# A decoder trunk on one core: gate-and-up operands built in place on VectorE, memory work at the head of the FFNs, other groups in the down projection

## The chip, the cores and the metric

The kernel runs on one core of one Trainium2 chip. The metric is the device time of one execution in microseconds; the time before is the median of three runs. Inputs and outputs are fp32.

## The reference

Two layers. Each has four sub-layers with an RMS norm before and after it: an FFN, a token mixer, a cross-attention into 256 memory tokens, and a second FFN. T is 512 tokens, the model width is 1024, the FFN's inner width 2816. Cut to what the change touches:

```python
def swiglu(x, w_gate, w_up, w_down):
    return (jax.nn.silu(x @ w_gate) * (x @ w_up)) @ w_down

for l in range(DEPTH):
    y = swiglu(rms_norm(x, ffn1_pre_g[l]), ffn1_w_gate[l], ffn1_w_up[l], ffn1_w_down[l])
    x = x + 0.5 * rms_norm(y, ffn1_post_g[l])
    y = hybrid_mixer(rms_norm(x, mix_pre_g[l]), ...)
    x = x + rms_norm(y, mix_post_g[l])
    y = memory_xattn(rms_norm(x, xa_pre_g[l]), rms_norm(mem, xa_mem_g[l]), ...)
    x = x + rms_norm(y, xa_post_g[l])
    y = swiglu(rms_norm(x, ffn2_pre_g[l]), ffn2_w_gate[l], ffn2_w_up[l], ffn2_w_down[l])
    x = x + 0.5 * rms_norm(y, ffn2_post_g[l])
```

## The kernel before, in words

**Layout and products.** All activations are kept transposed: eight tiles `x[0..7]` of 128 features by 512 tokens. An fp32 product is made of three matmuls in a rounded fp32 format: both operands are split into a high and a low part, and `mm3` (L119) adds high by high (L121), high weight by low x (L122) and low weight by high x (L123) in one PSUM bank. A weight unit is 128x1024: SyncE loads it raw, ScalarE copies the high part `whi` (L88), VectorE subtracts to get the low part `wlo` (L89). There are six raw buffers and four each of `whi` and `wlo`; four PSUM banks for accumulators and four for other uses.

**The FFN.** 22 blocks of 128 inner features are worked off as 11 pairs (class `Pair`, L325). Pairs 0 and 1 are plain: gate and up of each block, all eight x tiles (`plain`). Pairs 2 to 10 replace eight block products by seven, as Strassen's scheme does: the x side is cut into four blocks (two halves of the features by two halves of the tokens), and products 1 to 7 use x blocks or their differences and sums (operands `ops[o, k]`), with weight combinations that are loaded ready, or made by adding a second load onto the first: an accumulate-DMA issued on GpSimd's queue (L341, four per pair). The operands 1 to 4 are plain halves of x, 5 to 8 are built once per FFN in `combos` (L221), after the first plain pair: a 128x256 difference on VectorE, one on GpSimd, again one each, for four rows k; the high and low parts of operands 7 and 8 are made in a second loop over k. Their high parts have a buffer of their own, the rest comes from pool "xs" with 24 buffers.

The seven products run in the order p1, p5, p2, p7, p6, p4, p3. Each is 24 matmuls of 256 columns. Between them VectorE and GpSimd form the sums of the results: after p6 `e = B - s1` (L420, VectorE) and `s5 = e - s5` (L421, GpSimd); after p4 `s7 = e - s7` (L425) and `s5 = s5 - C` (L426), both on VectorE. `swiglu` then makes the gated product of both blocks and splits it (L132, L133).

**The down projection** goes in groups of blocks. When the list `hs` holds four finished blocks at the end of a pair's products, `down` runs them: for each of eight output tiles, 12 matmuls of 512 columns, and VectorE adds the bank to `y[c]` (L485). So groups of four run after pairs 2, 4, 6, 8 and 10, and a last group of two at the end. In the last FFN of the kernel the last group runs in two halves of 256 tokens (`down_halves`), so that the output of the first half leaves while the second is computed. In a last group the squares of y are added up as they come (`sumsq`, L161), on GpSimd for all tiles but the last, which is VectorE's.

**Between stages.** `postnorm` turns the sum of squares into a row of factors: a transposing matmul into `rms_ps` (L169), a reduction (L171), a short Newton iteration on VectorE in 128x4 operations (L139 to L148), a broadcasting matmul into `bc_ps` (L185). Then x is updated tile by tile and split anew for the next stage (`x1h`, L211). Where the next stage is an FFN, `postnorm` calls `nxt[0]()` first (L274): it runs that FFN's `filler`, if there is one (`mem_keys`, the cross-attention keys of the next layer, whose units run on TensorE as `ps_mk`), and splits the first two gate and up units. `ffn_first` (L446) makes this closure and leaves the pairs in `warm` for `ffn` (L457). Keys 0 to 3 of layer 1 ride ahead of ffn2 of layer 0, keys 4 to 7 ahead of ffn1 of layer 1.

**What sets the order.** A scheduler lists the instructions of each engine once, when the kernel is built, in the program's order as far as their inputs are ready in its own model; each engine then runs its list in order. A DMA is issued by the engine whose queue it is in, so an accumulate-DMA stands in GpSimd's list among its additions. A tile is reused when all that read it are done.

Of the kernel before, what the change touches and what calls it, by code (L numbers as in the profile page):

```python
# [9 lines left out]
F32 = mybir.dt.float32  # L10
F32R = mybir.dt.float32r
# [36 lines left out]
def trunk(ctx: ExitStack, tc: tile.TileContext, a: dict, out: bass.AP):  # L48
# [11 lines left out]
    def big(name, dt=F32, shape=(P, T), tag="b"):  # L60
        return bp.tile(list(shape), dt, name=name, tag=tag, bufs=slots[tag])
# [158 lines left out]

    def combos(g):  # L221

        sums = []
        h7 = big("x7h", F32R, shape=(P, 4, T), tag="onsa")

        def put(o, k, t, hi, lo):
            act.activation(hi, t, AF.Copy)
            dve.tensor_tensor(lo, t, hi.bitcast(F32), op=ALU.subtract)
            for u in range(2):
                ops[o + u, k] = hi[:, HALVES[u]], lo[:, HALVES[u]]  # L230

        for k in range(4):
            b = []
            for c in (k, k + 4):
                xg = big("xg")
                act.activation(xg, x[c], AF.Copy, scale=g[:, c : c + 1])
                b += [xg[:, HALVES[0]], xg[:, HALVES[1]]]
            t5, t7 = big("xt"), big("xt")
            dve.tensor_tensor(t5[:, :256], b[1], b[0], op=ALU.subtract)
            pool.tensor_tensor(t7[:, :256], b[3], b[1], op=ALU.subtract)  # L240
            dve.tensor_tensor(t5[:, 256:], b[3], t5[:, :256], op=ALU.subtract)
            pool.tensor_tensor(t7[:, 256:], t5[:, 256:], b[2], op=ALU.subtract)
            put(5, k, t5, big("x5h", F32R, tag="xs"), big("x5l", F32R, tag="xs"))
            sums.append(t7)
        for k in range(4):
            put(7, k, sums[k], h7[:, k], big("x7l", F32R, tag="xs"))

    def gcols(l, col):
        return small[l][:, col : col + NC]
# [20 lines left out]
    def postnorm(y, ssq, gains, nxt, ts_=slice(0, T), cols=None):  # L270


        w = ts_.stop - ts_.start
        if ts_.start == 0 and nxt[0]:  # L274
            nxt[0]()
        ps = row_bc(rms_cols(ssq[:, ts_], D, w, cols), w // P)
        for c in range(NC):
            t = big("yn")[:, :w]
            dve.scalar_tensor_tensor(t, y[c][:, ts_], gains[:, c : c + 1], ps, op0=ALU.mult, op1=ALU.mult)
            (dve if c == 0 else pool).tensor_tensor(x[c][:, ts_], x[c][:, ts_], t, op=ALU.add)  # L280
            (split_s if nxt[0] else split_x)(c, nxt[1], ts_)
# [16 lines left out]
    def out_halves(src, l, oh, ol, gains, nxt):  # L298

        y, ssq, w = [], None, {}  # L300
        for c in range(NC):
            wh, wl = unit(src[l, c], 1024)
            y.append(big("y"))
            if c >= NC - 2:
                w[c] = wh, wl
                continue
            ps = acc("ps_o")
            for k in range(NC):
                s = slice(k * P, (k + 1) * P)
                mm3(ps, wh[:, s], wl[:, s], oh[k], ol[k], k == 0, k == NC - 1)  # L310
            ssq = sumsq(ssq, ps, c, pool)
            dve.tensor_copy(y[c], ps)
        for ts_ in HALVES:
            for c in w:
                ps = acc("ps_o")[:, : T // 2]
                for k in range(NC):
                    s = slice(k * P, (k + 1) * P)
                    mm3(ps, w[c][0][:, s], w[c][1][:, s], oh[k][:, ts_], ol[k][:, ts_], k == 0, k == NC - 1)
                sq = big("sq")[:, : T // 2]
                act.activation(sq, ps, AF.Square)  # L320
                dve.tensor_tensor(ssq[:, ts_], ssq[:, ts_], sq, op=ALU.add)
                dve.tensor_copy(y[c][:, ts_], ps)
            postnorm(y, ssq, gains, nxt, ts_)

    class Pair:  # L325

# [118 lines left out]
    warm = {}  # L445

    def ffn_first(l, which, filler=None):

        def run():
            if filler:  # L450
                filler()
            ps_ = warm[l, which] = [Pair(a[FF_UNITS[which][0]][l], j) for j in range(NPAIR)]
            for q in range(2):
                ps_[0].w["q", q] = split_unit(ps_[0].load(q))
        return run

    def ffn(l, which, gains, nxt, prep=None):  # L457
        dn = FF_UNITS[which][1]
        pairs = warm.pop((l, which))
        y, state = [None] * NC, {"ssq": None}  # L460
        ORDER = "p1", "p5", "p2", "p7", "p6", "p4", "p3"

# [12 lines left out]
        def down(f0, hs, final):  # L475
            n = len(hs)
            for c, w in weights(f0, n):
                ps = acc("ps_dn")
                for k in range(n):
                    mm3(ps, *w[k], *hs[k], k == 0, k == n - 1)  # L480
                if f0 == 0:
                    y[c] = big("y")
                    act.activation(y[c], ps, AF.Copy)
                else:
                    dve.tensor_tensor(y[c], ps, y[c], op=ALU.add)  # L485
                if final:
# [7 lines left out]
        for p in pairs[:2]:  # L494
            for f in range(2):
                p.plain(f, bc, hs)
                if p is pairs[0] and f == 1:
                    combos(gcols(l, G_F1PRE if which == "ffn1" else G_F2PRE))
        f0 = 0
        for p in pairs[2:]:  # L500
            final = p is pairs[-1]
            for n in ORDER:
                getattr(p, n)()
            mine = []
            if len(hs) == 4:
                down(f0, hs, False)
                f0, hs = f0 + 4, []
            p.swiglu(bc, hs, "xs" if final else "h")
        if prep:
            prep()  # L510
        if nxt is None:
# [523 lines left out]
        mem_norm()  # L1035
        mem_split(0)

    ffn_first(0, "ffn1")()
    for c in range(NC):
        split_s(c, gcols(0, G_F1PRE))  # L1040
    ffn(0, "ffn1", half1[0], (None, gcols(0, G_MIXPRE)), prep=first_prep)
    mixer(0, (None, gcols(0, G_XAPRE)), filler=keys(0, 0, 7), prep=split_mem(0))
    xattn(0, (ffn_first(0, "ffn2", keys(1, 0, 4)), gcols(0, G_F2PRE)), filler=lambda: (mem_keys(0, 7, 8), mem_values(0, 0)), mid=values(0, 1), prep=split_mem(1))
    ffn(0, "ffn2", half2[0], (ffn_first(1, "ffn1", keys(1, 4, 8)), gcols(1, G_F1PRE)), prep=split_mem(1))
    ffn(1, "ffn1", half1[1], (None, gcols(1, G_MIXPRE)), prep=split_mem(1))
    mixer(1, (None, gcols(1, G_XAPRE)), filler=values(1, 0), prep=split_mem(1))
    xattn(1, (ffn_first(1, "ffn2"), gcols(1, G_F2PRE)), filler=values(1, 1), halves=True)
    ffn(1, "ffn2", half2[1], None)


# [90 lines left out]
```

## Time and profile before

| | us |
|---|---|
| median of three runs | 2546.82 (2544.16 to 2546.93) |
| the profiled execution | 2542.61 |
| its span, first to last instruction | 2540.8 |
| TensorE busy | 2402.8 |
| VectorE busy | 1696.1 |
| ScalarE busy | 1101.6 |
| GpSimd busy | 461.6 |

The profile is of one execution. A row of the timeline reads: start, duration, engine, line, operation, the tile written and those read, shapes and count; in brackets the time the engine sat idle before it and what ended that. PE is TensorE, DVE VectorE, ACT ScalarE, POOL GpSimd. PEclk is the granted clock of TensorE in tenths of full speed, 9 being 0.9 or more in a slice; in a table of stretches it is a share. Matmuls are pipelined: one row's duration is longer than the distance to the next.

### The profile page before, as it was taken

Reading aid. Unit: us, or ns where it says so; the run is one execution under the profiler, and the core shown is the slowest. Engines: PE = TensorE matmul, PEld = TensorE weight load, DVE = VectorE, ACT = ScalarE, POOL = GpSimd, SP = SyncE. Lnnn points to the kernel's source line nnn. Section 1 sums busy time; section 2 is a strip of 40 time slices with the busy share of each in tenths; the row PEclk is TensorE's granted clock in tenths of the full one; section 3 lists DMA queues with packets and bytes.
Section 4 is the critical chain, followed back from the end, with each engine's and each line's share of the span. In section 5 each row is a group of like instructions: output and inputs, shape, how many; then the busy total and the mean of one; then the engine's idle time right before and its main releaser. Section 6 shows DMA issues by size and latency. Waiting matters only on the chain.

```text
span 2540.8 us, 37896 instructions
## 1 busy us (share of the span) xinstructions
PE 2402.8 (95%) x14860; PEld 2132.7 (84%) x14860; DVE 1696.1 (67%) x3018; ACT 1101.6 (43%) x1760; POOL 461.6 (18%) x430
## 2 busy tenths in 40 slices
PE   8999988999999989999989999989999997999996
PEld 7999977888878879999879999868888776999995
DVE  7566687465777485666885666774657766756666
ACT  6443443255345354444454444422553443544442
POOL 2111123001040131111231111230010403211112
PEclk9999998999999999999989999989999998999998
DMA  6766642411232336666526666514112322367661
GB/s 209 166 161 163 165 151 67 143 51 52 74 104 95 100 78 164 164 160 159 160 80 163 167 167 160 149 58 142 51 51 68 100 67 75 98 162 166 165 163 35
DMA packets 107523, 309.59 MB, mean 122 GB/s; under 512 B 10448, under 2 KB 24016, under 8 KB 107344
## 3 DMA queue, kind: packets, MB, share of 16 engines
q1 hardware_dynamic: 77392, 222.21, 26.7%
q0 software_dynamic: 20736, 75.51, 17.7%
q10 hardware_dynamic: 9216, 9.44, 1.2%
q8 instruction: 117, 1.92, 0.3%
q14 instruction: 62, 0.51, 0.1%
HBM read 305.02 MB, written 2.10 MB: 121 GB/s over the span
## 4 chain that ended last, share of the span: by engine, by line
PE 43%; DVE 5%; issue 2%; DMA 2%; ACT 2%; POOL 1%; POOLq 0%; ACTq 0%; DVEq 0%
PE ps_gu L121 4%; PE ps_gu L122 4%; PE ps_gu L123 4%; PE ps_dn L121 3%; PE ps_dn L122 3%; PE ps_dn L123 3%; DMA raw<-in_ffn_gu_dram 2%; PE ps_po L829 1%; PE ps_gc L121 1%; PE ps_gc L123 1%; PE ps_gc L122 1%; PE ps_o L121 1%; PE ps_o L122 1%; PE ps_o L123 1%; PE ps_fm L123 1%
## 5 line engine op out<-in xcount | busy, mean ns | idle before, releaser
L89 DVE TENSOR_TENSOR wlo<-raw,whi 128x1024 fp32r<-128x1024 f32 (+1 forms) x506 | 619.7, 1231 | 410.6 <-ACT whi L88 408.2
L88 ACT ACTIVATE whi<-raw 128x1024 fp32r<-128x1024 f32 (+1 forms) x506 | 529.5, 1054 | 797.3 <-DMA raw<-in_ffn_gu_dram 185.5
L341 POOL DMA_DIRECT2D raw<-in_ffn_gu_dram x144 | 125.7, 891 | 974.9 <-DVE wlo L89 730.4
L121 PE MATMUL ps_dn<-hh,whi 128*128 128x512 f32 (+1 forms) x720 | 277.5, 385 | 1.2 <-DVE y L485 1.2
L122 PE MATMUL ps_dn<-hl,whi 128*128 128x512 f32 (+1 forms) x720 | 277.3, 385 | 0.0
L123 PE MATMUL ps_dn<-hh,wlo 128*128 128x512 f32 (+1 forms) x720 | 277.3, 385 | 0.0
L121 PE MATMUL ps_gu<-x3h,whi 128*128 128x256 f32 (+1 forms) x704 | 216.7, 308 | 24.9 <-ACT gk L375 24.9
L122 PE MATMUL ps_gu<-x3l,whi 128*128 128x256 f32 (+1 forms) x704 | 215.6, 306 | 1.2 <-DVE x3l L218 1.2
L161 POOL TENSOR_TENSOR ssq<-ssq,sq 128x512 f32<-128x512 f32 (+1 forms) x84 | 130.3, 1552 | 469.1 <-ACT sq L160 465.6
L123 PE MATMUL ps_gu<-x3h,wlo 128*128 128x256 f32 (+1 forms) x704 | 215.0, 305 | 0.0
L121 PE MATMUL ps_gu<-x1h,whi 128*128 128x256 f32 x544 | 158.1, 295 | 24.8 <-ACT x1h L211 11.0
L121 PE MATMUL ps_gc<-x7h,whi 128*128 128x256 f32 x576 | 163.3, 283 | 0.9 <-ACT gk L375 0.9
L121 PEld LDWEIGHTS ps_gu<-x3h,whi 128*128 128x128 f32 x704 | 136.6, 194 | 32.7 <-ACT gk L375 28.2
L121 PE MATMUL ps_gu<-x5h,whi 128*128 128x256 f32 x576 | 163.0, 283 | 0.0
L122 PE MATMUL ps_gu<-x5l,whi 128*128 128x256 f32 x576 | 163.0, 283 | 0.0
L123 PE MATMUL ps_gc<-x7h,wlo 128*128 128x256 f32 x576 | 163.0, 283 | 0.0
L122 PE MATMUL ps_gc<-x7l,whi 128*128 128x256 f32 x576 | 163.0, 283 | 0.0
L123 PE MATMUL ps_gu<-x5h,wlo 128*128 128x256 f32 x576 | 162.9, 283 | 0.0
L122 PE MATMUL ps_gu<-x1l,whi 128*128 128x256 f32 x544 | 158.6, 292 | 1.2 <-DVE x1l L212 1.0
L121 PEld LDWEIGHTS ps_dn<-hh,whi 128*128 128x128 f32 x720 | 135.5, 188 | 28.0 <-DVE y L485 1.6
L123 PEld LDWEIGHTS ps_dn<-hh,wlo 128*128 128x128 f32 x720 | 135.5, 188 | 27.1
L123 PE MATMUL ps_gu<-x1h,wlo 128*128 128x256 f32 x544 | 158.0, 292 | 0.2
(267 smaller groups left out, 5997.6 us busy)
## 6 DMA issues: line engine op xcount, KB each, us to landing
raw<-in_ffn_gu_dram SPq DMA_DIRECT2D x176, 512.0 KB, 4.1
raw<-in_ffn_gu_dram POOLq DMA_DIRECT2D x144, 512.0 KB, 5.7
raw<-in_ffn_dn_dram SPq DMA_DIRECT2D x88, 512.0 KB, 4.2
raw<-in_win_fm_dram SPq DMA_DIRECT2D x32, 512.0 KB, 3.6
raw<-in_wk_dram SPq DMA_DIRECT2D x16, 512.0 KB, 3.8
raw<-in_cmp_w_dram SPq DMA_DIRECT2D x16, 512.0 KB, 4.1
raw<-in_wout_dram SPq DMA_DIRECT2D x16, 512.0 KB, 3.3
raw<-in_wv_dram SPq DMA_DIRECT2D x16, 512.0 KB, 3.3
```

The costliest lines, as they stand in the source:

```text
L88: act.activation(hi, raw, AF.Copy)
L89: dve.tensor_tensor(lo, raw, hi.bitcast(F32), op=ALU.subtract)
L121: pe.matmul(ps, ah, bh, start=start, stop=False, skip_group_check=more)
L122: pe.matmul(ps, ah, bl, start=False, stop=False, skip_group_check=more)
L123: pe.matmul(ps, al, bh, start=False, stop=stop, skip_group_check=more)
L161: eng.tensor_tensor(acc_t, acc_t, sq, op=ALU.add)
L341: pool.dma_start(t, self.quarter(q), accum_op=ALU.add)
L829: pe.matmul(po[:, i], blk[i, j], vsel[j // 2][:, j % 2, col : col + DH], start=j == 0, stop=j == i)
```

## The change

- `combos`: all four differences of a row are made on VectorE and in place, in the two tiles that held the scaled x; the four blocks of the first tile become operands 5 and 7, those of the second 8 and 6. Both are split in the same turn of the loop, so no second loop.
- `p6`: `s5 = e - s5` is on VectorE.
- `ffn_first` and `warm` go; `ffn` takes the filler and runs it at its head, before its own norm rows, after the postnorm of the stage ahead. The splits of the first two units are made in `plain` like all others; the kernel's first two units alone are split ahead, through `cut`, among the first splits of x. The first entry of `nxt` becomes a flag for how x is split.
- The squares of a last group are added on VectorE for odd tiles and on GpSimd for even ones (not in `down_halves`).
- A down group also runs with two blocks in hand after pair 3, and, where another stage follows, after pair 10. So the groups of three FFNs are 4, 2, 4, 4, 4, 2, 2 (after pairs 2, 3, 5, 7, 9, 10 and at the end), and of the last FFN 4, 2, 4, 4, 4, 4, the last in halves.

```diff
 def combos(g):
-    sums = []
-    h7 = big("x7h", F32R, shape=(P, 4, T), tag="onsa")
-    def put(o, k, t, hi, lo):
-        act.activation(hi, t, AF.Copy)
-        dve.tensor_tensor(lo, t, hi.bitcast(F32), op=ALU.subtract)
-        for u in range(2):
-            ops[o + u, k] = hi[:, HALVES[u]], lo[:, HALVES[u]]
+    hb = big("x8h", F32R, shape=(P, 4, T), tag="onsa")
     for k in range(4):
...
-        t5, t7 = big("xt"), big("xt")
-        dve.tensor_tensor(t5[:, :256], b[1], b[0], op=ALU.subtract)
-        pool.tensor_tensor(t7[:, :256], b[3], b[1], op=ALU.subtract)
-        dve.tensor_tensor(t5[:, 256:], b[3], t5[:, :256], op=ALU.subtract)
-        pool.tensor_tensor(t7[:, 256:], t5[:, 256:], b[2], op=ALU.subtract)
-        put(5, k, t5, big("x5h", F32R, tag="xs"), big("x5l", F32R, tag="xs"))
-        sums.append(t7)
-    for k in range(4):
-        put(7, k, sums[k], h7[:, k], big("x7l", F32R, tag="xs"))
+        xg = [big("xg") for _ in range(2)]
+        for c, t in zip((k, k + 4), xg):
+            act.activation(t, x[c], AF.Copy, scale=g[:, c : c + 1])
+        b1, b2, b3, b4 = [t[:, u] for t in xg for u in HALVES]
+        for o, i, j in ((b1, b2, b1), (b2, b4, b2), (b4, b4, b1), (b3, b4, b3)):
+            dve.tensor_tensor(o, i, j, op=ALU.subtract)
+        for t, hi, o in ((xg[0], big("x5h", F32R, tag="xs"), (5, 7)), (xg[1], hb[:, k], (8, 6))):
+            lo = big("x5l", F32R, tag="xs")
+            act.activation(hi, t, AF.Copy)
+            dve.tensor_tensor(lo, t, hi.bitcast(F32), op=ALU.subtract)
+            for u in range(2):
+                ops[o[u], k] = hi[:, HALVES[u]], lo[:, HALVES[u]]
@@ postnorm
-    if ts_.start == 0 and nxt[0]:
-        nxt[0]()
@@ plain
-            k0 = "q", 2 * f + q
-            wh, wl = self.w.pop(k0) if k0 in self.w else split_unit(self.load(2 * f + q))
+            k0 = self.j, 2 * f + q
+            wh, wl = cut.pop(k0) if k0 in cut else split_unit(self.load(2 * f + q))
@@ p6
-        pool.tensor_tensor(self.s5, self.e, self.s5, op=ALU.subtract)
+        dve.tensor_tensor(self.s5, self.e, self.s5, op=ALU.subtract)
@@ ffn (ffn_first and warm are removed)
-def ffn(l, which, gains, nxt, prep=None):
+def ffn(l, which, gains, nxt, filler=None, prep=None):
+    if filler:
+        filler()
+    pairs = [Pair(a[FF_UNITS[which][0]][l], j) for j in range(NPAIR)]
...
-            state["ssq"] = sumsq(state["ssq"], y[c], c, dve if c == NC - 1 else pool)
+            state["ssq"] = sumsq(state["ssq"], y[c], c, dve if c % 2 else pool)
...
-        if len(hs) == 4:
+        if len(hs) == 4 or len(hs) == 2 and (p is pairs[3] or p is pairs[-1] and nxt is not None):
             down(f0, hs, False)
-            f0, hs = f0 + 4, []
+            f0, hs = f0 + len(hs), []
@@ the calls
-xattn(0, (ffn_first(0, "ffn2", keys(1, 0, 4)), gcols(0, G_F2PRE)), ...)
-ffn(0, "ffn2", half2[0], (ffn_first(1, "ffn1", keys(1, 4, 8)), gcols(1, G_F1PRE)), prep=split_mem(1))
-ffn(1, "ffn1", half1[1], (None, gcols(1, G_MIXPRE)), prep=split_mem(1))
+xattn(0, (True, gcols(0, G_F2PRE)), ...)
+ffn(0, "ffn2", half2[0], (True, gcols(1, G_F1PRE)), filler=keys(1, 0, 4), prep=split_mem(1))
+ffn(1, "ffn1", half1[1], (False, gcols(1, G_MIXPRE)), filler=keys(1, 4, 8), prep=split_mem(1))
```

## Rows read from the trace of the kernel before

**Rows 1.** The page: busy time of the engines, and granted clock in 40 slices.

```profile
PE 2402.8 (95%) x14860; PEld 2132.7 (84%) x14860; DVE 1696.1 (67%) x3018; ACT 1101.6 (43%) x1760; POOL 461.6 (18%) x430
...
PEclk9999998999999999999989999989999998999998
```

**Rows 2.** Waits of TensorE: us in total, times, longest us.

```profile
PE ps_gu L121 <- ACT gk L375: 24.9, 16, 2.3
PE bc_ps L185 <- DVE rs_y L148: 12.8, 11, 4.3
```

**Rows 3.** Stretches of 40 us at two changes of stage: busy us by engine, clock.

```profile
880.00:920.00 40.00, 30.90 (x200) 28.33 (x199) 31.89 (x48) 18.40 (x28) 16.01 (x11) 0.87 0.34 97
...
1280.00:1320.00 40.00, 31.18 (x182) 27.54 (x183) 33.94 (x65) 18.23 (x31) 16.22 (x12) 0.83 0.25 69
```

**Rows 4.** Timeline ahead of one wait of TensorE in pair 4 of an FFN.

```profile
1075.97 2.18 DVE L425 TENSOR_TENSOR gk<-ge,gk 128x512 f32<-128x512 f32 x1
1075.98 1.62 POOL L421 TENSOR_TENSOR gk<-ge,gk 128x512 f32<-128x512 f32 x1
...
1078.08 1.21 DVE L89 TENSOR_TENSOR wlo<-raw,whi 128x1024 fp32r<-128x1024 f32 x1
...
1079.60 0.88 POOL L341 DMA_DIRECT2D raw<-in_ffn_gu_dram  x1 [2.00 <-DVE wlo L89]
1079.82 1.21 DVE L89 TENSOR_TENSOR wlo<-raw,whi 128x1024 fp32r<-128x1024 f32 x1
...
1085.48 1.06 ACT L88 ACTIVATE whi<-raw 128x1024 fp32r<-128x1024 f32 x1 [2.20 <-DMA raw<-in_ffn_gu_dram]
...
1088.12 0.39 PE L121 MATMUL ps_gu<-x3h,whi 128*128 128x256 f32 x1 [2.13 <-ACT gk L375]
```

**Rows 5.** VectorE's subtraction L425: min/median/max ns; its sum, mean; the wait for L421.

```profile
L425 DVE TENSOR_TENSOR gk<-ge,gk x36: 678/1739/2198, 72.8 to 2476.4; 128x512 f32<-128x512 f32 x36
...
L425 DVE TENSOR_TENSOR gk<-ge,gk 128x512 f32<-128x512 f32 x36 | 52.0, 1444 | 0.5
...
  POOL gk L421: 37.1, 15
```

**Rows 6.** Accumulate-DMA issues on GpSimd's queue: duration of an issue, min/median/max ns.

```profile
L341 POOL DMA_DIRECT2D raw<-in_ffn_gu_dram x144: 862/865/1197, 29.7 to 2466.5; - x144
```

**Rows 7.** Timeline from the last square to the first gate product of ffn2, layer 0.

```profile
882.89 0.68 DVE L161 TENSOR_TENSOR ssq<-ssq,sq 128x512 f32<-128x512 f32 x1
...
892.20 0.60 PE L169 MATMUL rms_ps<-cst,ssq 128*128 128x128 f32 x4
...
900.32 1.01 PE L121 MATMUL ps_gu<-x1h,whi 128*128 128x256 f32 x3 [2.64 <-ACT x1h L211]
```

**Rows 8.** The same ahead of ffn1, layer 1.

```profile
1269.79 0.69 DVE L161 TENSOR_TENSOR ssq<-ssq,sq 128x512 f32<-128x512 f32 x1 [1.19 <-POOL ssq L161]
...
1277.66 0.60 PE L169 MATMUL rms_ps<-cst,ssq 128*128 128x128 f32 x4
...
1288.10 1.23 PE L121 MATMUL ps_gu<-x1h,whi 128*128 128x256 f32 x4 [4.16 <-ACT x1h L211]
```

**Rows 9.** Timeline of the last group in halves, and the wait behind it.

```profile
2502.77 0.28 PE L121 MATMUL ps_dn<-hh,whi 128*128 128x256 f32 x1
...
2514.96 0.28 PE L123 MATMUL ps_dn<-hh,wlo 128*128 128x256 f32 x1
...
2518.50 0.72 ACT L160 ACTIVATE sq<-y 128x256 f32<-128x256 f32 x2 [6.87 <-POOL x L532]
...
2527.02 0.69 PE L169 MATMUL rms_ps<-cst,ssq 128*128 128x128 f32 x2 [10.38 <-DVE ssq L161]
```

**Rows 10.** Gating of pair 10 in the last FFN: its first sum and its last copy.

```profile
2481.19 0.69 DVE L431 TENSOR_TENSOR ge<-ps_gu,ge 128x512 f32<-128x512 f32 x1 [0.17 <-PE ps_gu L123]
...
2490.43 0.63 ACT L132 ACTIVATE hh<-g 128x512 fp32r<-128x512 f32 x1 [2.81 <-DVE g L442]
```

**Rows 11.** A wait of TensorE for a weight split in the first mixer.

```profile
403.98 0.58 PE L123 MATMUL ps_mk<-memg,wlo 128*128 128x256 f32 x1 [3.10 <-DVE wlo L89]
```

More of the change, by code (lines that the diff above doesn't have):

```diff
@@ L221, in combos @@
     def combos(g):
-        sums = []
-        h7 = big("x7h", F32R, shape=(P, 4, T), tag="onsa")
-        def put(o, k, t, hi, lo):
-            act.activation(hi, t, AF.Copy)
-            dve.tensor_tensor(lo, t, hi.bitcast(F32), op=ALU.subtract)
-            for u in range(2):
-                ops[o + u, k] = hi[:, HALVES[u]], lo[:, HALVES[u]]
-        for k in range(4):
[L233 to L237, printed above, removed]
-            t5, t7 = big("xt"), big("xt")
-            dve.tensor_tensor(t5[:, :256], b[1], b[0], op=ALU.subtract)
-            pool.tensor_tensor(t7[:, :256], b[3], b[1], op=ALU.subtract)
-            dve.tensor_tensor(t5[:, 256:], b[3], t5[:, :256], op=ALU.subtract)
-            pool.tensor_tensor(t7[:, 256:], t5[:, 256:], b[2], op=ALU.subtract)
-            put(5, k, t5, big("x5h", F32R, tag="xs"), big("x5l", F32R, tag="xs"))
-            sums.append(t7)
-        for k in range(4):
-            put(7, k, sums[k], h7[:, k], big("x7l", F32R, tag="xs"))
+        hb = big("x8h", F32R, shape=(P, 4, T), tag="onsa")
+        for k in range(4):
+            xg = [big("xg") for _ in range(2)]
[10 more added lines that the diff above has]
+                    ops[o[u], k] = hi[:, HALVES[u]], lo[:, HALVES[u]]
     def gcols(l, col):
@@ L323, in out_halves @@
             postnorm(y, ssq, gains, nxt, ts_)
+    cut = {}
     class Pair:
@@ L443, in swiglu @@
                 hs.append(split(g1, "h", 0.5, tag=tag))
[L445 to L455, printed above, removed]
-    def ffn(l, which, gains, nxt, prep=None):
+    def ffn(l, which, gains, nxt, filler=None, prep=None):
+        if filler:
+            filler()
+        pairs = [Pair(a[FF_UNITS[which][0]][l], j) for j in range(NPAIR)]
         dn = FF_UNITS[which][1]
-        pairs = warm.pop((l, which))
         y, state = [None] * NC, {"ssq": None}
@@ L496, in ffn @@
                 p.plain(f, bc, hs)
-                if p is pairs[0] and f == 1:
-                    combos(gcols(l, G_F1PRE if which == "ffn1" else G_F2PRE))
+            if p is pairs[0]:
+                combos(gcols(l, G_F1PRE if which == "ffn1" else G_F2PRE))
         f0 = 0
         for p in pairs[2:]:
-            final = p is pairs[-1]
             for n in ORDER:
                 getattr(p, n)()
-            mine = []
-            if len(hs) == 4:
+            if len(hs) == 4 or len(hs) == 2 and (p is pairs[3] or p is pairs[-1] and nxt is not None):
                 down(f0, hs, False)
-                f0, hs = f0 + 4, []
-            p.swiglu(bc, hs, "xs" if final else "h")
+                f0, hs = f0 + len(hs), []
+            p.swiglu(bc, hs, "xs" if p is pairs[-1] else "h")
         if prep:
@@ L1036, in first_prep @@
         mem_split(0)
-    ffn_first(0, "ffn1")()
-    for c in range(NC):
+    cut[0, 0] = split_unit(first.pop((0, 0)))
+    for c in range(4):
         split_s(c, gcols(0, G_F1PRE))
-    ffn(0, "ffn1", half1[0], (None, gcols(0, G_MIXPRE)), prep=first_prep)
-    mixer(0, (None, gcols(0, G_XAPRE)), filler=keys(0, 0, 7), prep=split_mem(0))
-    xattn(0, (ffn_first(0, "ffn2", keys(1, 0, 4)), gcols(0, G_F2PRE)), filler=lambda: (mem_keys(0, 7, 8), mem_values(0, 0)), mid=values(0, 1), prep=split_mem(1))
-    ffn(0, "ffn2", half2[0], (ffn_first(1, "ffn1", keys(1, 4, 8)), gcols(1, G_F1PRE)), prep=split_mem(1))
-    ffn(1, "ffn1", half1[1], (None, gcols(1, G_MIXPRE)), prep=split_mem(1))
-    mixer(1, (None, gcols(1, G_XAPRE)), filler=values(1, 0), prep=split_mem(1))
-    xattn(1, (ffn_first(1, "ffn2"), gcols(1, G_F2PRE)), filler=values(1, 1), halves=True)
+    cut[0, 1] = split_unit(first.pop((0, 1)))
+    for c in range(4, NC):
+        split_s(c, gcols(0, G_F1PRE))
+    ffn(0, "ffn1", half1[0], (False, gcols(0, G_MIXPRE)), prep=first_prep)
+    mixer(0, (False, gcols(0, G_XAPRE)), filler=keys(0, 0, 7), prep=split_mem(0))
+    xattn(0, (True, gcols(0, G_F2PRE)), filler=lambda: (mem_keys(0, 7, 8), mem_values(0, 0)), mid=values(0, 1), prep=split_mem(1))
+    ffn(0, "ffn2", half2[0], (True, gcols(1, G_F1PRE)), filler=keys(1, 0, 4), prep=split_mem(1))
+    ffn(1, "ffn1", half1[1], (False, gcols(1, G_MIXPRE)), filler=keys(1, 4, 8), prep=split_mem(1))
+    mixer(1, (False, gcols(1, G_XAPRE)), filler=values(1, 0), prep=split_mem(1))
+    xattn(1, (True, gcols(1, G_F2PRE)), filler=values(1, 1), halves=True)
     ffn(1, "ffn2", half2[1], None)
```

## The prediction

> **What bounds the kernel now.** I read the page's busy shares first: TensorE is busy 95% of the span, VectorE 67%, GpSimd 18% [rows 1]. So only what leaves TensorE waiting, or what adds to its work, can move the time: 2540.8 − 2402.8 = 138 us of the span is idle TensorE. The slice line shows that the granted clock is at 0.8 to 0.9 in a few slices, which are the changes of stage. Then the waits of TensorE: the largest group is the gate and up product that waits for ScalarE's copy of a PSUM bank, 24.9 us in 16 waits; the normalisation's last VectorE step costs another 12.8 us in 11 [rows 2]. Then stretches of 40 us around the stage changes: 30.9 and 31.2 us of TensorE in 40, at a granted clock of 0.87 and 0.83, with VectorE at 32 and 34 us [rows 3]. There VectorE is nearly as full as TensorE. Last the timelines around each.
>
> **Rows 4 are one of the 16 waits, followed back.** TensorE stops for 2.13 us at 1088.12. The product it starts needs a PSUM bank that ScalarE frees late, because ScalarE had waited 2.20 us for an accumulated weight tile (1085.48). That tile's accumulate-DMA was issued by GpSimd at 1079.60, after VectorE's split at 1078.08, and that split stood behind one VectorE subtraction that took 2.18 us beside a GpSimd subtraction of 1.62 us. Alone the same subtraction takes 0.68 us; its mean is 1.44 [rows 5]. All 16 waits come at the third product of pairs 4, 6, 8 and 10, each of them after a pair at whose end no down group ran: a down group gives the loads 22 us of slack, a pair without one gives none.
>
> **The change part by part.** *(1) s5 on VectorE.* 36 subtractions leave GpSimd. VectorE takes on 36 × 0.68 = 24 us and loses what the collision cost it, 36 × (1.44 − 0.68) = 27 us [rows 5]. Its waits for the GpSimd result, 37.1 us in 15 [rows 5], go. So VectorE's load is about even and its delay smaller: in the chain of rows 4 the split comes 2.18 − 0.68 = 1.5 us earlier, less 0.68 if the moved subtraction stands ahead of it, so 0.8 to 1.5 earlier. How much of a wait of 1.55 us (24.9 / 16) that takes is open, since the DMA's landing (5.9 us from issue to use here) varies too: 0 to all of it; I take a third, 0.5 us. Nothing on GpSimd queues behind anything then: between the accumulate issues its list is empty.
>
> The Trainium skill, page "SBUF — State Buffer", section "SBUF: two separate sides", says that VectorE (with two SBUF inputs) and GpSimd share a port pair as an exclusive lock, and that a DMA issued from GpSimd's queue can be starved of its descriptors while VectorE holds it. Its first half agrees with the 2.18 us above; its second half speaks against this part, since it puts another two-input VectorE operation beside the accumulate issues. The trace of before doesn't show that: the issue at 1079.60 took 0.88 us beside the split of 1079.82, which reads two SBUF tiles, and over all 144 the median is 0.865 and the longest 1.197 [rows 4, 6]. By the rule each of some 12 waits would be up to 0.68 us longer, +8 us, and the sum would come to 2531; by the rows it stays.
>
> *(2) Down groups.* 22 blocks went as 4,4,4,4,4,2 after pairs 2, 4, 6, 8, 10 and the end. Now three FFNs go 4,2,4,4,4,2,2, after pairs 2, 3, 5, 7, 9, 10 and the end, and the last goes 4,2,4,4,4 and then 4 in halves. So "two blocks larger" holds for the last group of the last FFN alone. Pairs without a group before them are then 5, 7 and 9 in an FFN: three waits in place of four, and 4 × 1.55 = 6.2 us go. With part 1's 12 × 0.5 = 6 the sum is **−12**, bounds 0 (the waits only move) and −25 (all go). The number of weight loads is the same; the extra group adds 8 y additions, 8 × 0.68 = 5.5 us of VectorE beside a TensorE that runs.
>
> The other side of it is the end of the first three FFNs. After the last product, the block's gating takes from 2481.19 to the copy at 2490.43, some 10.6 us with the second split behind it, and today hides under a group of four blocks, 2481 to 2502.8, 21.8 us [rows 9, 10]. After the change it has a group of two, 10.9 us, in which VectorE must do 8 y additions instead of the 4 that half of the longer group brings, 4 × 0.68 = 2.7 us more. So the last group waits 10.6 + 2.7 − 10.9 = 2.4 us in each: **+7**, bounds 0 and +15 (5 each: the preparation of the next stage queues there too).
>
> *(3) Memory work to the head of FFNs.* Of the key work, 96 matmuls run between out-projection and the transpose of ffn2(0)'s post-norm. The sum of squares is ready at 883.6 and its transpose runs at 892.20 only, so 8.6 us are lost; the first gate product starts at 900.32 after waits of 4.3 (the normalisation, the longest of [rows 2]) and 2.64 us [rows 7]. At the head of the FFN, the transpose goes at 883.7 and the same matmuls can fill the waits behind it. What then is late is VectorE: the splits of the key weights and of the first gate units, 1.22 us each, come behind the norm instead of beside the matmuls, and four of these units' worth, less what the norm leaves open, is 2.5 us. I take 8.5 − 2.5 = **−6**, bounds 0 and −8.5. Before ffn1(1) it's the same: ready at 1270.5, transpose at 1277.66, first product at 1288.10 after 4.16 [rows 8]; 7.2 less 2.2 is **−5**, bounds 0 and −7.2. The last FFN had no such matmuls: 0 ± 3 there.
>
> *(4) Tail.* In the last FFN the final group of two in halves lasts from 2502.77 to 2515.2. The second half's squares wait 6.87 us on ScalarE for buffers that the first half's output still holds, and the transpose comes 10.38 us after the last product [rows 9]. With halves of four blocks the second half lasts 11.5 us instead of 5.8, the output of the first ends within it, and the transpose comes some 2 to 2.5 us after the last product, −8 to −9.5 with a little shorter queue. Against it: the last group no longer hides pair 10's gating, which without y additions (2.7) and weight splits (two, 2.4) lasts 10.6 − 5.1 = 5.5 us. The blocks of pair 9 give 24 matmuls that can go before, in four PSUM banks, at 0.12 us each 2.9 us; so 2.6 are lost, and I add 1 for a lower clock after the wait, as the slices at stage changes have it. **−5.5**, bounds −9.5 and +3.
>
> *(5) Differences in place.* Eight subtractions of 128x256 per FFN move from GpSimd to VectorE; not over 0.68 us each [rows 5], 5.5 us per FFN, beside the matmuls of the plain pairs. The third and fourth block rows get buffers that the first pair frees; by my count they're ready 4 us before product 5 wants them. **0**; without that cover one wait per FFN, of 2 us as in rows 4, +8. *(6) Squares alternate in the final group*: the VectorE addition at 1269.79 [rows 8] waited 1.19 us for GpSimd; it's in the −5. *(7) The start* is the same work in nearly the same order: **0**.
>
> Sum against the profiled execution (2542.6, span 2540.8 and 1.8 around it): −12 + 7 − 6 − 5 − 5.5 = −21.5, so 2521.1. That execution lies 4.2 under the median of the runs, 2546.8; a median of after may lie either way, so I add half: **2523 us**.
>
> **The rivals.** *A. VectorE becomes the bound at stage changes (slower).* It is at 34 us of 40 there already [rows 3], and where in an earlier stage such splits queued behind the norm, TensorE waited 3.10 us in one place [rows 11]. Then the transitions give 0, the ends of FFNs cost their +15, each of 12 waits becomes 1.55 + 0.68 = 2.2 (26.9 in place of 24.9, +2), and only the tail's −5.5 stays: +11.5, **2556**. It decides where the last group's second block is split over 5 us after TensorE wants it. Against it: VectorE's total hardly grows.
>
> *B. The moved memory matmuls were no cost.* If the chain of normalisation and not TensorE's order sets the start of the next FFN, the transitions give 0: −10.5, **2534**. For it: after the transpose the wait is VectorE's. Against: the sum of squares stands ready 8.6 and 7.2 us.
>
> *C. The groups do not do what their name says and the waits move only.* In three of four FFNs the last group stays at two blocks, and the one ahead of it shrinks. If pairs 5, 7 and 9 wait as long in sum as 4, 6, 8 and 10 did and the transitions give a quarter, the sum is 0 + 7 − 2.8 − 5.5 = −1.3, **2543**.
>
> *D. All waits of rows 4 vanish*, because only the collision made the load late: −25 in place of −12: 2508 to 2510, **2509**.
>
> **How the numbers follow.** My forecast, 2512 to 2534, has 0.53; D 0.11, B 0.10, C 0.12 and A 0.14. A difference under 0.2% (5 us) can't be told from none: C lies there, and so does the upper edge of B. Faster is 0.53 + 0.11 + 0.09 (of B) = 0.73, within it 0.01 + 0.12 = 0.13, slower 0.14. The range runs from 2503, just under D, to 2553, into A.
>
> **What would show it.** Part 1: VectorE's subtraction at 0.68 us throughout, no waits for GpSimd's, and the group of 16 waits shrinks to 12 under 1.1 us each, at pairs 5, 7, 9; wrong if the sum stays at 25. Part 2: a wait for the split of the last block just ahead of each final group, 2 to 3 us in three FFNs; A if over 5. Part 3: the transpose within 1 us of the sum of squares, the first gate product of ffn2(0) and ffn1(1) 5 to 6 us earlier counted from the last product before; B if not. Part 4: the end comes about 16 us after the last product, not 25.6. The prediction is wrong if VectorE stands full beside an idle TensorE for over 10 us at any of these places, or if the first seven-product pair waits for its differences.

## The result, and the profile after

The changed kernel takes 2521.57 us, median of four runs (2520.18 to 2530.73), against 2545.88 for the kernel before beside it (2544.16 to 2546.93): ratio 0.9913, interval 0.9888 to 0.9937. The forecast was 2523. The profiled execution took 2522.7, span 2520.9. A second set on another chip gives 2517.92 against 2539.74, 0.9917 (0.9903 to 0.9930); that kernel is called *changed again* below.

The page of the changed kernel, busy shares, and then its waits of TensorE (columns as in [rows 1, 2]); the last line is the group that led, in *changed again*:

```profile
PE 2405.7 (95%) x14908; PEld 2134.0 (85%) x14908; DVE 1703.9 (68%) x3119; ACT 1102.9 (44%) x1760; POOL 368.5 (15%) x353
```

```profile
PE ps_gu L121 <- ACT gk L365: 12.3, 12, 1.9
...
PE rms_ps L169 <- DVE ssq L161: 7.5, 3, 3.7
...
PE bc_ps L185 <- DVE rs_y L148: 4.3, 9, 2.3
```

```profile
PE ps_gu L121 <- ACT gk L365: 9.7, 12, 1.7
```

TensorE does 3 us more work than before and VectorE 8 us more; what went is idle time. The group that led the waits [rows 2] is halved, 24.9 us in 16 to 12.3 in 12, and the norm's step to a third. To see where the rest went, I cut each execution at marks that all have: the first matmul of product 7 in an FFN, its last down product, and the end. This is worked out from TensorE's rows in the timelines; the columns are the kernel before, the changed one, the changed one again, and a variant of the experiments (4,4,4,4,4,2 in the first three FFNs):

| stretch, us | before | changed | again | variant |
|---|---|---|---|---|
| start to product 7 of ffn1, layer 0 | 66.0 | 67.6 | 67.1 | 66.1 |
| to product 7 of ffn2, layer 0 | 896.4 | 887.8 | 885.8 | 884.3 |
| to its last down product | 303.9 | 296.3 | 295.5 | 297.5 |
| to product 7 of ffn1, layer 1 | 81.8 | 84.8 | 83.1 | 78.3 |
| to its last down product | 300.9 | 295.8 | 295.7 | 296.7 |
| to product 7 of ffn2, layer 1 | 564.9 | 566.9 | 567.0 | 566.9 |
| to its last down product | 301.4 | 304.2 | 303.3 | 303.5 |
| to the end | 25.6 | 17.6 | 17.5 | 17.5 |
| span | 2540.8 | 2520.9 | 2515.0 | 2510.7 |

The FFNs gain. The tail gains 8 us, and the last FFN ahead of it gives back 2.8 in the table, 5.1 once the waits of the third product, which got shorter there too, are taken off. One row runs against the forecast: the change of stage from ffn2 of layer 0 to ffn1 of layer 1 got longer.

The subtraction that had met GpSimd's now takes the same time in all 36 pairs (columns as in [rows 5]), and an accumulate issue what it took before [rows 6]:

```profile
L415 DVE TENSOR_TENSOR gk<-ge,gk x36: 684/686/689, 74.9 to 2471.2; 128x512 f32<-128x512 f32 x36
...
L331 POOL DMA_DIRECT2D raw<-in_ffn_gu_dram x144: 865/865/1222, 31.1 to 2460.6; - x144
```

The change of stage to ffn2 of layer 0 in the changed kernel, TensorE's rows (against [rows 7]): the transpose no longer stands behind the 96 memory matmuls, which fill the time to the broadcast, and the first gate product comes 14.1 us after the last product (878.45) instead of 19.5 (880.85).

```profile
881.33 0.63 PE L169 MATMUL rms_ps<-cst,ssq 128*128 128x128 f32 x4
887.71 0.62 PE L185 MATMUL bc_ps<-cst,rs_y 128*128 128x128 f32 x4
892.51 0.50 PE L121 MATMUL ps_gu<-x1h,whi 128*128 128x256 f32 x2 [1.20 <-ACT x1h L211]
```

The change to ffn1 of layer 1 in the changed kernel (against [rows 8]), TensorE and VectorE, the last line being the broadcast in the kernel before. The last down product ends at 1251.67. The last addition to y comes at 1255.58, the last square at 1258.09, and then the steps of the norm stand between weight splits on VectorE: from transpose to broadcast 11.5 us, where the kernel before took 5.2 (in *changed again* it is 10.0).

```profile
1255.58 0.68 DVE L465 TENSOR_TENSOR y<-ps_dn,y 128x512 f32<-128x512 f32 x1
1256.18 1.98 DVE L89 TENSOR_TENSOR wlo<-raw,whi 128x1024 fp32r<-128x1024 f32 x1
1258.09 0.68 DVE L161 TENSOR_TENSOR ssq<-ssq,sq 128x512 f32<-128x512 f32 x1
1258.82 0.66 PE L169 MATMUL rms_ps<-cst,ssq 128*128 128x128 f32 x4 [2.48 <-DVE ssq L161]
1262.93 0.16 DVE L175 TENSOR_SCALAR rms_v<-rms_s 128x4 f32<-128x4 f32 x1
1263.00 1.22 DVE L89 TENSOR_TENSOR wlo<-raw,whi 128x1024 fp32r<-128x1024 f32 x1
1264.13 0.16 DVE L139 TENSOR_SCALAR rs_i<-rms_v 128x4 int32<-128x4 int32 x1
...
1265.92 1.23 DVE L89 TENSOR_TENSOR wlo<-raw,whi 128x1024 fp32r<-128x1024 f32 x1 [0.47 <-ACT whi L88]
...
1270.28 0.65 PE L185 MATMUL bc_ps<-cst,rs_y 128*128 128x128 f32 x4 [2.48 <-DVE rs_y L178]
1275.09 1.22 PE L121 MATMUL ps_gu<-x1h,whi 128*128 128x256 f32 x4 [4.16 <-ACT x1h L211]
```

```profile
1282.82 1.12 PE L185 MATMUL bc_ps<-cst,rs_y 128*128 128x128 f32 x4 [4.56 <-DVE rs_y L178]
```

In the 30 us behind that last product TensorE is idle for 10.0 us in the changed kernel, with VectorE busy in 8.7 of them; in the kernel before it is 8.7 and 7.1, counted from its last product at 1266.31.

And its tail (against [rows 9]): the two waits for pair 10's gating ahead of the last group, and the transpose 3.75 us after the last product instead of 10.38.

```profile
2478.94 0.39 PE L121 MATMUL ps_dn<-hh,whi 128*128 128x256 f32 x1 [1.49 <-DVE g L432]
2482.73 0.73 PE L121 MATMUL ps_dn<-hh,whi 128*128 128x256 f32 x4 [0.84 <-ACT hh L132]
...
2507.08 0.69 PE L169 MATMUL rms_ps<-cst,ssq 128*128 128x128 f32 x2 [3.75 <-DVE ssq L161]
```

### The profile page after: what moved, and what is told of

It is laid out like the page before. It is cut to its first block, busy times and chain, and to the rows that moved or that the text cites. A ratio compares the mean times of both kernels' runs of the same rounds, so it can differ in the third digit from the quotient of the medians.

```text
span 2520.9 us, 37910 instructions
## 1 busy us (share of the span) xinstructions
PE 2405.7 (95%) x14908; PEld 2134.0 (85%) x14908; DVE 1703.9 (68%) x3119; ACT 1102.9 (44%) x1760; POOL 368.5 (15%) x353
## 4 chain that ended last, share of the span: by engine, by line
PE 68%; DVE 11%; issue 5%; DMA 3%; ACT 3%; POOL 1%; POOLq 0%; ACTq 0%; DVEq 0%
PE ps_gu L121 6%; PE ps_gu L122 6%; PE ps_gu L123 6%; PE ps_dn L121 4%; PE ps_dn L122 4%; PE ps_dn L123 4%; PE ps_po L807 3%; DMA raw<-in_ffn_gu_dram 2%; PE ps_o L121 2%; PE ps_o L122 2%; PE ps_o L123 2%; PE ps_gc L123 2%; PE ps_gc L122 2%; PE ps_gc L121 2%; PE ps_fm L123 2%
## 5 line engine op out<-in xcount | busy, mean ns | idle before, releaser
L121 PE MATMUL ps_gu<-x3h,whi 128*128 128x256 f32 (+1 forms) x704 | 214.4, 305 | 12.3 <-ACT gk L365 12.3
L161 POOL TENSOR_TENSOR ssq<-ssq,sq 128x512 f32<-128x512 f32 (+1 forms) x75 | 114.7, 1530 | 484.8 <-ACT sq L160 405.0
L121 PE MATMUL ps_gu<-x1h,whi 128*128 128x256 f32 x544 | 158.2, 294 | 24.9 <-ACT x1h L211 9.6
L465 DVE TENSOR_TENSOR y<-ps_dn,y 128x512 f32<-128x512 f32 x176 | 119.8, 689 | 70.1 <-PE ps_dn L123 69.9
L122 PE MATMUL ps_gc<-x5l,whi 128*128 128x256 f32 x576 | 163.0, 283 | 0.0
L122 PEld LDWEIGHTS ps_dn<-hl,whi 128*128 128x128 f32 x736 | 138.5, 188 | 25.7 <-DVE hl L133 0.4
L122 PEld LDWEIGHTS ps_gu<-x3l,whi 128*128 128x128 f32 x704 | 134.6, 191 | 7.0 <-DVE x3l L218 2.7
L123 PEld LDWEIGHTS ps_gu<-x3h,wlo 128*128 128x128 f32 x704 | 134.5, 191 | 5.0
```

The costliest lines, as they stand in the source:

```text
L121: pe.matmul(ps, ah, bh, start=start, stop=False, skip_group_check=more)
L122: pe.matmul(ps, ah, bl, start=False, stop=False, skip_group_check=more)
L123: pe.matmul(ps, al, bh, start=False, stop=stop, skip_group_check=more)
L161: eng.tensor_tensor(acc_t, acc_t, sq, op=ALU.add)
```

## The experiments

All ratios are to the kernel before on the same chip. First each part was taken back from the changed kernel, beside a kernel before of 2540.93 us; by 0.9913 to 0.9917 the changed kernel would be at 2519 to 2520 there.

**s5 back on GpSimd.**

```diff
-            dve.tensor_tensor(self.s5, self.e, self.s5, op=ALU.subtract)
+            pool.tensor_tensor(self.s5, self.e, self.s5, op=ALU.subtract)
```

> The changed kernel (2521.6 us) with s5 = e - s5 back on GpSimd, all else as changed. Theory (the collision makes the split and the accumulated load late): VectorE's next subtraction takes about 1.4 us in the mean again instead of 0.69, the 12 waits of the third product for ScalarE's copy grow from 12.3 us in all towards 12 x 1.55 = 18.6, with a dip of the granted clock after the longest, so +6 to +9: 2528 to 2531 us. Rival (the other grouping of the down blocks alone made the waits fewer and shorter): the waits stay at 12 to 13 us and the time at 2520 to 2523.

Measured 2526.67 us, 0.9951 (0.9939 to 0.9963). Its 12 waits, and the subtraction:

```profile
PE ps_gu L121 <- ACT gk L365: 18.2, 12, 2.0
```

```profile
L415 DVE TENSOR_TENSOR gk<-ge,gk x36: 681/1741/2200, 74.6 to 2479.0; 128x512 f32<-128x512 f32 x36
```

The waits are close to the theory's 18.6, the collision is back, and some 8 us are lost (0.9951 against 0.9913 to 0.9917). The rival falls.

**The groups of before.**

```diff
-            if len(hs) == 4 or len(hs) == 2 and (p is pairs[3] or p is pairs[-1] and nxt is not None):
+            if len(hs) == 4:
```

> The changed kernel with the down groups of before (4,4,4,4,4,2 in all FFNs). Theory: 16 waits instead of 12, of about 1.0 us each as now, so 16 to 17 us (+4); the end of the last FFN gets its long wait for the squares back, and its last group hides the gating again (+3 net); the ends of the other three FFNs give 0: together +7, 2528 to 2529 us. Rival (the forecast's term for the FFN ends): the three ends get 2.4 us back each, so +4 + 3 - 7 = 0, 2521 to 2522.

Measured 2515.79 us, 0.9900 (0.9886 to 0.9915): neither 2528 nor 2521, but no slower than the changed kernel, rather faster. Its interval overlaps that of the changed kernel. The waits are 14.4 us instead of 12.3, and the tail is the long one, as expected; but the change of stage to ffn1 of layer 1 takes 78.3 us instead of 84.8. So the small groups do cost, as the forecast had it, at a place where the forecast had none: behind the last group, not ahead of it.

```profile
PE ps_gu L121 <- ACT gk L365: 14.4, 16, 2.8
```

**The memory work ahead of the postnorm again**, with the splits of the first two units:

```diff
+        if ts_.start == 0 and len(nxt) > 2:
+            nxt[2]()
         ps = row_bc(rms_cols(ssq[:, ts_], D, w, cols), w // P)
...
+    def ahead(l, which, filler=None):
+        def run():
+            if filler:
+                filler()
+            for q in range(2):
+                cut[0, q] = split_unit(raw_unit(a[FF_UNITS[which][0]][l][0, q], 1024))
+        return run
...
-    ffn(0, "ffn2", half2[0], (True, gcols(1, G_F1PRE)), filler=keys(1, 0, 4), prep=split_mem(1))
+    ffn(0, "ffn2", half2[0], (True, gcols(1, G_F1PRE), ahead(1, "ffn1", keys(1, 4, 8))), prep=split_mem(1))
```

> The changed kernel with the memory work and the splits of the first two units ahead of the postnorm again (ffn2 of layer 0, ffn1 and ffn2 of layer 1). Theory from the two traces: the change of stage to ffn2 of layer 0 loses its 4.6 us, the one to ffn1 of layer 1 gets 3.3 us back, the third is the same: +1.3, 2523 us. Rival (the forecast: both gained, 6 and 5): +11, 2532 to 2533.

Measured 2519.80 us, 0.9923 (0.9909 to 0.9936): the theory's 2523 can't be told from no change, and the forecast's 2532 falls. In the changed kernel as a whole this part is worth little. Of the theory's two places one held: the change to ffn2 of layer 0 loses 4.7 us. The one to ffn1 of layer 1 was to get 3.3 us back and got 0.9 (83.9 us, against 84.8 and, in *changed again*, 83.1), though the transpose there has no wait again. TensorE, with the last product at 1252.90:

```profile
1264.69 0.60 PE L169 MATMUL rms_ps<-cst,ssq 128*128 128x128 f32 x4
1269.94 1.12 PE L185 MATMUL bc_ps<-cst,rs_y 128*128 128x128 f32 x4 [4.65 <-DVE rs_y L178]
1275.56 1.23 PE L121 MATMUL ps_gu<-x1h,whi 128*128 128x256 f32 x4 [4.50 <-ACT x1h L211]
```

**The squares of before.**

```diff
-                    state["ssq"] = sumsq(state["ssq"], y[c], c, dve if c % 2 else pool)
+                    state["ssq"] = sumsq(state["ssq"], y[c], c, dve if c == NC - 1 else pool)
```

> The changed kernel with the squares of the last group on GpSimd for all tiles but the last. Theory 1 (alternating shortens the chain of squares by 1 to 2 us at each of three ends): +3 to +5, 2525 to 2527 us, the sum of squares later after the last down product. Theory 2 (at the change to ffn1 of layer 1, where the sum of squares comes 7.1 us after the last product instead of 4.2, the VectorE additions are what is late): -3 there and about -3 in all, 2518 to 2519.

Measured 2524.35 us, 0.9939 (0.9926 to 0.9951), some 5 us slower: theory 1. From the last down product of ffn1 of layer 1 to the second transpose behind it, that of the mixer's own norm, this kernel takes 38.4 us, the changed one 35.2 and the kernel before 33.5 (TensorE's rows). The alternation takes back a good part of what the small groups cost there, but not all. At the change to ffn1 of layer 1, theory 2's place, it takes 82.2 us; executions of this stretch without that edit take 82.5 (the run with s5 back on GpSimd) to 84.8, so theory 2 isn't shown there.

Then four beside a kernel before of 2539.74 us, the first being the changed kernel itself.

> The changed kernel itself once more, as the measure for its neighbours on the same chip: ratio 0.991 to 0.992 to the kernel before.

2517.92 us, 0.9917. Its waits came to 9.7 us instead of 12.3 in the first profile: such a sum moves by some 2 to 3 us between executions of one kernel.

**The kernel before with s5 on VectorE alone** (the one line above, the other way).

> The kernel before with one edit alone: s5 = e - s5 on VectorE. Theory (the collision of the two subtractions makes the weight load late): the 16 waits of the third product fall from 24.9 us to about 16 x 0.9 = 14 to 16 us, the dips of the granted clock behind the longest go, so -9 to -14, ratio 0.9945 to 0.9965. Rival (the waits come from the missing down group, whatever VectorE does): they stay at 22 to 25 us, ratio 0.999 to 1.000. Third possibility (the starved accumulate-DMA): waits over 25 us, ratio over 1.001.

Measured 2525.87 us, 0.9954 (0.9940 to 0.9967).

```profile
PE ps_gu L121 <- ACT gk L375: 11.1, 16, 1.7
```

All 16 waits are there, without any new group, but of 0.7 us instead of 1.55. This part alone gives about 12 us by the ratio (14 by the medians). The third possibility, a starved accumulate-DMA, falls with it.

**The small groups in the last FFN alone.**

```diff
-            if len(hs) == 4 or len(hs) == 2 and (p is pairs[3] or p is pairs[-1] and nxt is not None):
+            if len(hs) == 4 or len(hs) == 2 and p is pairs[3] and nxt is None:
```

> The changed kernel with the groups 4,2,4,4,4,4 in the last FFN alone and 4,4,4,4,4,2 in the other three. Theory (two small groups at the end leave VectorE no room, so the sum of squares and the norm behind it come late): the three stage changes behind an FFN get 2.6, 6.5 and 2.5 us back, three waits more of 1 us or so; the last FFN and the tail as changed: some 4 to 7 us under the changed kernel, ratio 0.9885 to 0.990. Rival (the gain seen with the groups of before is scatter between executions): within 2 us of the changed kernel.

Measured 2512.01 us (2506.5 to 2513.05), 0.9889 (0.9875 to 0.9903), below every run of the changed kernel beside it (2516.61 to 2519.47). It is the fastest found. TensorE at the change to ffn1 of layer 1, where the last product ends at 1247.86:

```profile
1252.06 0.66 PE L169 MATMUL rms_ps<-cst,ssq 128*128 128x128 f32 x4 [1.21 <-DVE ssq L161]
1258.51 0.65 PE L185 MATMUL bc_ps<-cst,rs_y 128*128 128x128 f32 x4 [0.17 <-DVE rs_y L178]
1263.34 0.62 PE L121 MATMUL ps_gu<-x1h,whi 128*128 128x256 f32 x3 [1.31 <-ACT x1h L211]
```

Transpose 4.2 us, broadcast 10.7 and first gate product 15.5 us after the last product; in the changed kernel 7.1, 18.6 and 23.4. VectorE's busy time in the 22 us ahead of the last product goes with it (the third engine column), first this variant, then the changed kernel:

```profile
1225.86:1247.86 22.00, 22.00 (x100) 18.23 (x99) 17.32 (x26) 11.19 (x18) 2.29 (x2) 1.00 0.48 146
```

```profile
1229.67:1251.67 22.00, 22.00 (x98) 17.92 (x97) 20.76 (x36) 11.48 (x19) 1.30 (x1) 1.00 0.43 131
```

20.8 of 22 us against 17.3: VectorE was nearly full under a TensorE that had no wait, and so it carried additions and squares over the end. It is 20.7 to 22.0 us in each of the seven traces with two small groups at that end, 16.3 to 17.5 in the five with a group of four and one of two, and 19.9 in the next run.

**4,2,4,4,4,4 in all FFNs.**

```diff
+            if len(hs) == 4 or len(hs) == 2 and p is pairs[3]:
```

> The changed kernel with the groups 4,2,4,4,4,4 in all four FFNs (the last in one piece where a stage follows). Theory: the y additions come 2.7 us apart again, so the sum of squares comes about 4 us after the last product and the stage changes get their 2.6 to 6.5 us back as with the groups of before; but nothing hides the gating of pair 10, a wait of 2.3 us as in the last FFN, three times, with a lower clock behind it; the waits of the third product stay at 12. Net -2 to -5 against the changed kernel. Rival (what is late is the gating itself, that every grouping has to wait for): the last group waits over 4 us each and the time is +2 or more against the changed kernel.

Measured 2513.53 us, 0.9900 (0.9886 to 0.9913), 4.4 under the changed kernel. The change to ffn1 of layer 1 takes 78.0 us, and 12 waits come to 7.3 us, not the theory's 12. A last group of four with nothing to hide the gating is better than two small ones, and the rival falls. But the theory's price for it did not show: of its three waits of 2.3 us for the gating there is one, of 0.46 us, in ffn1 of layer 0.

```profile
PE ps_gu L121 <- ACT gk L365: 7.3, 12, 1.1
```

Last, beside a kernel before of 2540.35 us:

**The kernel before with the new groups alone** (the condition of the changed kernel).

> The kernel before with the new groups of the down projection alone (4,2,4,4,4,2,2 in three FFNs, 4,2,4,4,4,4 in the last). Theory: 12 waits instead of 16 of about 1.55 us as before, 24.9 to 18 or 19 us (-6); the tail as in the changed kernel (-4 to -5 with the wait for the gating in it); the three stage changes behind an FFN lose 2.6 to 6.5 us each, as measured between the two groupings with the changed kernel, +11: in all 0 to +3, ratio 0.999 to 1.001. Rival (the forecast's terms -6, -5.5, +7): -4.5, ratio 0.998.

Measured 2536.12 us, 0.9981 (0.9970 to 0.9992): the theory of 0 to +3 falls, the sum by the forecast's terms, −4.5, holds. The waits are 17.2 us in 12 (the line below). And the change to ffn1 of layer 1 takes 81.9 us, as in the kernel before (81.8): here the small groups cost nothing. TensorE there, with the last product at 1263.80:

```profile
PE ps_gu L121 <- ACT gk L375: 17.2, 12, 2.1
```

```profile
1275.15 0.60 PE L169 MATMUL rms_ps<-cst,ssq 128*128 128x128 f32 x4
1280.35 1.11 PE L185 MATMUL bc_ps<-cst,rs_y 128*128 128x128 f32 x4 [4.61 <-DVE rs_y L178]
```

The transpose has no wait: it stands behind the memory matmuls, as before, and the late squares are done in their shadow. At the change to the mixer of layer 1, which has no such matmuls ahead of its transpose, the small groups do cost here too: its second transpose comes 37.4 us after the last down product instead of 33.5.

**The kernel before with the memory work at the head alone.**

```diff
+    def ffn(l, which, gains, nxt, filler=None, prep=None):
+        if filler:
+            filler()
```

> The kernel before with the memory work at the head of the FFNs alone, the splits of the first two units in their place after it. Theory (TensorE's order was what held the transpose back): the transpose follows the sum of squares within 1 us; the change of stage to ffn2 of layer 0 gives 4.5, that to ffn1 of layer 1 3.5, as between the kernel before and the changed one with the old groups: -8, ratio 0.9968. Rival (the norm's chain or VectorE sets it): 0 to -2, ratio 0.999 to 1.000.

Measured 2531.12 us, 0.9967 (0.9956 to 0.9979): the theory, with an interval of 3 us to either side. The change to ffn1 of layer 1 takes 78.2 us, 3.5 less; TensorE there, with the last product at 1256.99, transpose 4.2 and broadcast 10.7 us after it:

```profile
1261.19 0.66 PE L169 MATMUL rms_ps<-cst,ssq 128*128 128x128 f32 x4 [1.22 <-DVE ssq L161]
1267.64 0.65 PE L185 MATMUL bc_ps<-cst,rs_y 128*128 128x128 f32 x4 [0.16 <-DVE rs_y L178]
1272.48 0.62 PE L121 MATMUL ps_gu<-x1h,whi 128*128 128x256 f32 x3 [1.31 <-ACT x1h L211]
```

**The differences of before.**

> The changed kernel with the differences of before (two on VectorE, two on GpSimd per row, operands 7 and 8 split last). Theory (hidden beside the plain pairs both ways): within 2 us of the changed kernel, ratio 0.991 to 0.992. Rival (GpSimd's subtractions slow VectorE's splits, or the last operands come late for the first seven-product pair): +2 to +8, with a wait of TensorE at the fifth or seventh product of pair 2.

Measured 2517.99 us, 0.9912 (0.9898 to 0.9925): nothing, either way; no wait at products 5 or 7 of pair 2.

By their ratios, s5, the groups and the memory work are worth 11.7, 4.8 and 8.4 us alone on the kernel before, 24.9 in sum, each within some 3 us. Together, with the differences in place, which are worth nothing, they are the run with the squares of before: 15.5 us. So they don't add up; the 9 us between are more than these intervals give (some 6). The squares bring 5 to 6 of them back.

## Why the prediction came out right, step by step

The sum was right, in part by luck. Some terms held; of the others two misses of like size cancelled: the clock behind the waits, 5.1 us that stood in no term, and the change of stage to ffn1 of layer 1, forecast at −5 and a third of +7, so −2.7, and measured at +3.0 (+1.4 in *changed again*).

*Waits of the third product, −12.* Measured −12.6 (12.3 left; 9.7 in the second execution). But they were put together wrongly: 6.2 for the fourth wait and 0.5 for each of twelve. Alone, s5 on VectorE takes 24.9 to 11.1, 0.86 a wait; the groups alone to 17.2. Both together do little more than the first, 9.1 to 12.3 in five executions, since each acts on the same late load. Rival D's mechanism was more than half true. The sign of waits under 1.1 us each failed: four of the twelve are 1.3 to 1.9.

What the term left out is the clock. Stretches of the kernel before, from the end of a wait on; the third figure from the right is the granted clock, as a share of full speed:

```profile
1088.00:1096.00 8.00, 7.88 (x53) 7.88 (x54) 4.73 (x7) 3.61 (x6) 0.86 (x1) 0.79 0.56 134
...
1154.00:1162.00 8.00, 7.79 (x53) 7.79 (x54) 4.77 (x7) 3.68 (x6) 0.86 (x1) 0.79 0.59 134
...
1600.00:1610.00 10.00, 9.81 (x69) 9.82 (x70) 6.02 (x8) 4.82 (x7) 0.86 (x1) 0.83 0.55 115
```

0.79 is a mean of time at 1.2 and time at 2.4 GHz, and costs 0.21 × 8 = 1.7 us; with the third, 5.1 us. In the changed kernel the stretches behind its longest waits (1.3 to 1.9 us) are at 1.00. In ffn2 of layer 0 the waits fell by 4.1 us and the FFN by 7.6; the two dips, 3.4, are the rest.

*The rule on the shared port.* The Trainium skill, "SBUF — State Buffer", section "SBUF: two separate sides", has a VectorE operation with two SBUF inputs and a GpSimd operation that reads SBUF lock each other out. The 1741 ns median beside GpSimd and the 686 without agree. But the Trainium skill tells in that section of starved DMA issues for VectorE's two-port modes, and not for a subtraction of two inputs. So the +8 us that the prediction drew from it was more than the section says. The rows of this kernel show nothing of it either: an issue took 0.865 us in the median before and after, and the waits got shorter.

*Ends of three FFNs, +7.* Near as a sum, wrong as a place. The second split of pair 10 did come about as late as forecast, 2.2 to 2.3 us into the last group of each of the three FFNs; in ffn2 of layer 0 the group starts at the first of these rows and the low part of the split ends at 1242.71:

```profile
1240.38 0.39 PE L121 MATMUL ps_dn<-hh,whi 128*128 128x512 f32 x1
1242.02 0.69 DVE L133 SCALAR_TENSOR_TENSOR hl<-g,hh 128x512 fp32r<-128x512 f32 x1
```

Yet no last group waited for it: the first block's matmuls ran ahead into free PSUM banks, which I had counted in the tail and not here. The 2.7 us of extra additions per end were real; they came out behind the last product, where at ffn2 of layer 0 the last addition to y starts 3.9 us after it in the changed kernel and 0.9 in the variant: as late squares and a norm that shares VectorE with splits. The changed kernel again and the variant of the table ran on one chip: its rows 2, 4 and 6 differ by 1.5, 4.9 and 0.1 us, 6.5 together. Of these the 4.9 alone is more than two executions of one kernel differ by; and row 2 also holds the variant's fourth wait.

*Memory work, −6 and −5.* The first measured −4.6 from the last out-projection product to the transpose of the FFN's own norm, which stands behind the memory matmuls in both kernels (42.2 to 37.5), and the first gate product came 5.4 us earlier, as the sign had it. The second is −3.5 alone and +3.0 in the changed kernel (+1.4 in the second execution); its first gate product comes 23.4 us after the last product (21.7 in the second execution) instead of 21.8, so that sign failed. The step that failed is that the two edits were added. With the old groups the memory work at the head gains 3.5 us here, and the small groups cost 0.1 while the memory matmuls stand ahead; with both edits the gain is gone and VectorE's lateness is bare. That was rival A's mechanism, at one of its places, with VectorE busy in 8.7 of 10.0 idle us of TensorE, under the 10 that the prediction had named. That the memory matmuls were the cover of the late squares is what the runs on the kernel before say; in the changed kernel, putting them back brought only 0.9 us, so the cover isn't all of it, and the rest stays open.

*Tail, −5.5.* Measured −2.9: last FFN and tail, less the waits of the third product, are 317.9 us in the changed kernel and 320.8 in it with the old groups. The two parts hold: 8.0 off the end (8 to 9.5), 2.3 of waiting (2.6). The clock, priced at 1, stayed at 1.00; instead the last FFN is 2.8 us longer beside its waits, which no term had. Most of that lies in the last group: by TensorE's rows it takes 28.2 us, less 2.3 of waiting, against 23.0 for its 192 matmuls of 0.12 us, with the first half's transposes and broadcast within it.

*Squares.* Cost at 1.2 within another term; they are worth some 5 us, by the run that takes them back: with the small groups VectorE's chain of squares would come later still.

*Differences in place, 0.* Held. *Start, 0.* The first product waited 7.7 us for its weights in the profile before and 9.2 in the one after; with an unchanged start it is 7.7 to 9.9 over the executions of these kernels, so this is scatter.

What stays open: the mixer and cross-attention of layer 0 lost some 2 us in the changed profile, which no run singled out.

## What to carry to other kernels

Where two engines work on the two halves of one small step, look at the spread of one operation's duration: 0.68 to 2.2 us told of the collision, and a move to the engine that already had more to do was worth 12 us. Two edits that are each right can take one another's gain away; ask of each what the other needs, and run each alone and both. And an engine that is full under a busy TensorE shows no wait until TensorE's work ends: read its busy time in the stretch ahead of the change of stage.

## What the hardware showed that was not expected

The granted clock fell behind three waits of the kernel before (2.01, 2.13 and 2.22 us; means of 0.79 to 0.83 over 8 to 10 us), and not behind two others of the same size (2.27 and 2.03), whose stretches are these:

```profile
127.00:137.00 10.00, 9.31 (x77) 9.31 (x78) 6.77 (x10) 5.64 (x9) 0.86 (x1) 1.00 0.53 115
2275.00:2285.00 10.00, 9.74 (x81) 9.74 (x82) 6.69 (x11) 5.64 (x8) 0.86 (x1) 1.00 0.53 120
```

So a wait of 2 us in the middle of dense matmuls cost now 2 and now nearly 4. Over all thirteen traces of this case, 24 waits of the third product lasted more than 1.70 us, and behind 14 of them the clock fell; behind the 151 shorter ones it never did. That none of the changed kernel's waits shows a fall, its longest of 1.9 us included, is then partly luck.

Sums of such waits moved by 2 to 3 us between two executions of the changed kernel (12.3 and 9.7), and the first load by 2 us; differences of that size between two single profiles say nothing.
